# An emission planner with measured durations, a latency per engine, and turns for VectorE and GpSimd

## The chip, the core and the metric

The kernel runs on one core of one Trainium2 chip. The metric is the device time of one execution in microseconds (us), as the median of several runs. Five engines work side by side, each through a queue of its own in the order in which the program was emitted: TensorE (PE in the profile; its weight loads are PEld), VectorE (DVE), ScalarE (ACT), GpSimd (POOL) and SyncE (SP), which here issues the transfers. An instruction waits, by semaphores, for what it reads and for the buffer that it writes, and everything behind it on its queue waits with it.

## The reference

A model of one block of a first kind and two layers of a second kind, on 512 tokens of 1024 columns, all in float32. Cut to what matters here:

```python
def first_block(x, p, ...):
    z = rmsnorm(x, mix_norm) @ w_in                     # 1024 -> 5120
    y_a = pool_mixer(z[..., :1024]) @ w_branch_a        # means over 2, 4, 8, 16 tokens
    y_b = spatial_gating(z[..., 1024:3072]) @ w_branch_b
    x = x + (g_a * y_a + g_b * y_b) @ w_out             # g: sigmoids of the rest of z
    x = x + conv_ffn(rmsnorm(x, ffn_norm), ...)         # 1024 -> 2 x 2816 -> 1024, conv of width 3
    x = x + sigmoid(rmsnorm(x, ple_norm) @ w_ple_gate) * (p @ w_ple)
    return rmsnorm(x, final_norm)

def second_block(x, ...):
    for i in range(2):
        x = x + 0.5 * swiglu(rmsnorm(x, ...), ...)      # 1024 -> 2 x 2816 -> 1024
        h = rmsnorm(x, mix_norm[i])
        x = x + (sliding_window_attention(h, ...) if i == 0 else latent_attention(h, ...))
        x = x + 0.5 * swiglu(rmsnorm(x, ...), ...)
    return x
```

`sliding_window_attention` adds to its scores a bias that depends on the distance of two positions (a table of 32 rows, picked by thresholds). `latent_attention` has 16 heads of 96 columns and a causal mask.

## The kernel before

**Numbers.** Activations lie with columns on partitions and the 512 tokens on the free axis. Each float32 operand is split into two parts that TensorE multiplies exactly (`op`, high and low; `wh` and `wl` for a weight), and a product takes three matmuls for each block of 128 x 128 weights: `wh` with the high part, `wh` with the low part, `wl` with the high part. A projection of 1024 columns to 128 is 8 blocks, 24 matmuls of 512 columns, into one PSUM bank. There are five banks `ps` for these and three banks `pt` for small products.

**Weights** come in chunks of 128 x 1024: a transfer on SP into `wr` (3 buffers), a cast on ScalarE to `wh` and a subtraction on GpSimd to `wl` (4 buffers each, so that three chunks are ahead of the one in use).

**Stages.** `mixer`; `conv_ffn`; `ple`; `final_and_ffn` (the last norm of the first block and a feed-forward); `attn_a` (sliding window); two times `ffn`; `attn_b` (latent); `ffn`. A feed-forward goes through `up_down`: 12 pairs of projections with what stands between them and the operand of the down projection (in `conv_ffn`: a convolution of three tokens for each of the two, a gelu, a product and a split), `down(0)` over the first 11 hidden blocks, 10 pairs, `down(1)` over the other 11. Eleven blocks are 33 matmuls for each of the 8 banks of a down projection.

**A norm** begins with ScalarE's squares of the eight tiles of `x` and VectorE's sum over them (`sumsq`, additions f<-f of two SBUF tiles). TensorE then takes the column sums with `mcol` (four float32 products of one column, `mean_tok`), VectorE makes the reciprocal root from them in twelve small steps and a diagonal matrix, TensorE a product of it with `ones`, and ScalarE copies that (`bcast`). Projections of the stage can start before, since the factor of a token is applied to their result.

**The table of biases** for the sliding window is made during `conv_ffn` in 28 chunks (`plan_bias`, `step`), one with each pair where any are left: two times three instructions on VectorE (`e` from `poshi`, `e` with `poslo`, `g` with `poslo`), 24 small matmuls into a `pt` bank, two additions of the mask `con` on VectorE, and, for each second chunk, stores on SP.

**The order.** The program is traced once with stand-ins; each operation becomes an `Instr` with its dependences and its buffers. `Order.arrange` then plays the program through in time: each engine has a clock, an operation can start when its inputs are done, `LAT` = 150 ns later, and its buffers are free, and of those that can start an engine takes the one that is earliest in the program. `_cost` gives the duration of each. A pool's tag in `SPARE` (`f` 3, `ps` 3, `e` 2) may be taken out of the program's order only while so many buffers more than needed are free; with fewer, it is handed out in the program's order. What comes out is the emission order, and with it each engine's queue. The instruction that the profile names L586 is the one line that emits everything. The costs on which the diff bears are

```python
                return max(n / 2.4 + 0.5, 56.0)
        return (3.4 if o.name == "tensor_copy" else 2.24) * n + 80
```

the first for a matmul of n columns on split operands, the second for GpSimd.

Of the kernel before, what the change touches and what calls it, by code (L numbers as in the profile page):

```python
# [10 lines left out]
F32 = mybir.dt.float32  # L11
# [27 lines left out]
SPARE = {"f": 3, "ps": 3, "e": 2}  # L39


# 1 / (2 pi) in parts of 11 bits
# [7 lines left out]
# ---------------------------------------------------------------- host layout  # L50
# [200 lines left out]
# ------------------------------------------------------------- issue order  # L251
#
# The program is first traced with tiles and views that stand for the real ones,
# then every engine's instructions are put in the order in which a list schedule
# over rough costs would start them, and emitted so.
# [99 lines left out]
class Instr:  # L355
    __slots__ = ("eng", "name", "args", "kw", "deps", "tiles", "cost", "new", "table", "n", "ready", "bytes", "key",
                 "rows")
# [10 lines left out]
class Order:  # L368
    LAT = 150.0
# [13 lines left out]
    def _cost(self, o):  # L383
# [3 lines left out]
        if o.eng == "tensor":  # L387
            if o.name == "transpose":
                return 107.0
            n = math.prod(kw["rhs"].shape[1:])  # L390
            dt = kw["rhs"].dtype
            if dt == F32R:
                return max(n / 2.4 + 0.5, 56.0)
            return 4 * (n / 2.4 + 2.5) if dt == F32 else max(n / 2.4 + 2.5, 27.0)
# [18 lines left out]
        return (3.4 if o.name == "tensor_copy" else 2.24) * n + 80  # L413

    def add(self, eng, name, args, kw):
# [29 lines left out]
        o.cost = self._cost(o)  # L445
        o.rows = kw["rhs"].shape[0] / P if "rhs" in kw else 1.0
# [7 lines left out]
    def arrange(self):  # L454
        import heapq
# [17 lines left out]
        warm, busy, window = False, 0.0, 0.0  # L473
# [8 lines left out]
        def fits(o):  # L482
# [5 lines left out]
            for k, c in need.items():  # L488
                if free[k] < c:
                    return False  # L490
                if free[k] < c + SPARE.get(k[1], 99):
                    f, i = fifo[k], head[k]
                    while c:
                        if id(f[i]) not in placed:
                            if f[i] not in o.new:
                                return False
                            c -= 1
                        i += 1
            return True

        while len(out) < len(self.ops):
# [8 lines left out]
            for e in engines:  # L510
# [44 lines left out]
                clock[e] = now + c  # L555
                end = now + c
# [5 lines left out]
                for x in after[o.n]:  # L562
                    x.ready = max(x.ready, end + (0.0 if x.eng == o.eng == "tensor" else self.LAT))
# [8 lines left out]
            if not nxt:  # L572
                if progress:
                    continue
                stuck = [(e, self.ops[n].name, n, [b.name for b in self.ops[n].new]) for e in engines
                         for _, n in sorted(able[e])[:2]]
                raise RuntimeError(f"no order found: {stuck}")
            now = min(nxt)
        return out
# [10 lines left out]
# ---------------------------------------------------------------- on the chip  # L590
# [37 lines left out]
class Core:  # L628
# [80 lines left out]
    # products of operands in two exact parts  # L709
# [84 lines left out]
    # ------------------------------------------------------------ first block  # L794
# [211 lines left out]
    # ----------------------------------------------------------- second block  # L1006
# [32 lines left out]
    # relative-position bias and mask of the sliding window, one table entry at  # L1039
    # a time by thresholds of the distance  # L1040
# [80 lines left out]
    def attn_a(self):  # L1121
# [13 lines left out]
        # heads of 64 columns brought to length one, in place  # L1135
# [34 lines left out]
        # keys of the two groups side by side, zero where the groups do not meet  # L1170
# [116 lines left out]
    # sine and cosine of position times frequency, by exact reduction in turns  # L1287
# [62 lines left out]
    def attn_b(self):  # L1350
# [7 lines left out]
        # latents and the shared key part, tokens on partitions, two token tiles at a time  # L1358
# [50 lines left out]
        # one over the length of four heads of 96 columns in four token tiles  # L1409
# [79 lines left out]
        # keys of tile st against queries st..3, three banks  # L1489
# [154 lines left out]
```

## Time and profile before

| | |
|---|---|
| median of 3 runs | 2785.83 us (2784.25 to 2788.27) |
| span of the profiled execution | 2782.1 us |
| TensorE busy | 2679.4 us, 96 % of the span |
| VectorE, ScalarE, GpSimd busy | 1376.1, 954.7, 1225.4 us (49, 34, 44 %) |
| read from memory | 242.76 MB, 91 GB/s over the span with what is written |

The profile is of one execution. Its span is the time from the first to the last instruction. Busy time is the time in which an engine works on something; waiting for a semaphore is idle. PEclk is the granted clock of TensorE as a share of its upper level: 1.00 is 2.4 GHz and 0.50 is 1.2 GHz. An arrow in a row is out<-in, by the tiles' names; the shape is partitions x elements.

### The profile page before, as it was taken

Reading aid. Unit: us, or ns where it says so; the run is one execution under the profiler, and the core shown is the slowest. Engines: PE = TensorE matmul, PEld = TensorE weight load, DVE = VectorE, ACT = ScalarE, POOL = GpSimd, SP = SyncE. Lnnn points to the kernel's source line nnn. Section 1 sums busy time; section 2 is a strip of 40 time slices with the busy share of each in tenths; the row PEclk is TensorE's granted clock in tenths of the full one; section 3 lists DMA queues with packets and bytes.
Section 4 is the critical chain, followed back from the end, with each engine's and each line's share of the span. In section 5 each row is a group of like instructions: output and inputs, shape, how many; then the busy total and the mean of one; then the engine's idle time right before and its main releaser. Section 6 shows DMA issues by size and latency. Waiting matters only on the chain. (4 is left out here: it accounts for less than half of the span.)

```text
span 2782.1 us, 32524 instructions
## 1 busy us (share of the span) xinstructions
PE 2679.4 (96%) x12768; PEld 2187.3 (79%) x12768; DVE 1376.1 (49%) x2193; ACT 954.7 (34%) x1486; POOL 1225.4 (44%) x664
## 2 busy tenths in 40 slices
PE   7999998999799899999999999999999899999999
PEld 5788886888677788889778888888888766688887
DVE  5506369949937861335743313343133676533141
ACT  3324333323334222334633223323223475432221
POOL 4543443353334344444534444444444443344443
PEclk9999999999899999999999999999999999999999
DMA  4232223333323333333222233322333201233322
GB/s 148 95 99 89 93 92 102 93 114 106 91 70 97 99 99 98 99 99 105 78 84 93 97 99 99 97 86 97 98 99 96 58 12 31 72 99 99 98 92 83
DMA packets 102617, 254.31 MB, mean 91 GB/s; under 512 B 37360, under 2 KB 39024, under 8 KB 102464
## 3 DMA queue, kind: packets, MB, share of 16 engines
q1 hardware_dynamic: 101840, 250.26, 28.4%
q8 instruction: 101, 1.65, 0.2%
q0 software_dynamic: 624, 1.97, 0.2%
q14 instruction: 52, 0.43, 0.1%
HBM read 242.76 MB, written 9.44 MB: 91 GB/s over the span
## 5 line engine op out<-in xcount | busy, mean ns | idle before, releaser
L586 PE MATMUL ps<-op,wh 128*128 128x512 f32 x6624 | 2069.9, 393 | 35.9 <-ACT op L586 24.4
L586 POOL TENSOR_TENSOR wl<-wr,wh 128x1024 fp32r<-128x1024 f32 (+3 forms) x467 | 1107.6, 2374 | 1393.3 <-ACT wh L586 1380.0
L586 PEld LDWEIGHTS ps<-op,wh 128*128 128x128 f32 x6624 | 1250.5, 189 | 304.7 <-ACT op L586 27.0
L586 PE MATMUL ps<-op,wl 128*128 128x512 f32 x3312 | 1299.7, 392 | 0.0
L586 ACT CAST wh<-wr 128x1024 fp32r<-128x1024 f32 (+3 forms) x471 | 468.1, 994 | 1236.7 <-PE ps L586 760.4
L586 PEld LDWEIGHTS ps<-op,wl 128*128 128x128 f32 x3312 | 627.4, 189 | 132.2 <-issue 1.0
L586 DVE TENSOR_TENSOR f<-ps,f 128x512 f32<-128x512 f32 x260 | 178.8, 688 | 532.9 <-PE ps L586 510.9
L586 DVE TENSOR_TENSOR op<-f,op 128x512 fp32r<-128x512 f32 x136 | 226.2, 1665 | 68.8 <-ACT op L586 68.0
L586 DVE TENSOR_TENSOR f<-f 128x512 f32<-128x512 f32 x213 | 203.1, 954 | 46.0 <-POOL f L586 19.8
L586 DVE SCALAR_TENSOR_TENSOR x<-ps,x 128x512 f32<-128x512 f32 x64 | 44.2, 691 | 339.0 <-PE ps L586 339.0
L586 ACT CAST op<-f 128x512 fp32r<-128x512 f32 x136 | 84.2, 621 | 211.1 <-DVE f L586 211.1
L586 PE MATMUL ps<-wh,op 128*128 128x256 f32 (+3 forms) x608 | 149.9, 333 | 4.8 <-ACT f L586 2.5
L586 PEld LDWEIGHTS ps<-wh,op 128*128 128x128 f32 x608 | 106.0, 194 | 15.6 <-ACT f L586 3.1
L586 ACT ACTIVATE f<-f 128x512 f32<-128x512 f32 x142 | 89.0, 627 | 77.8 <-DVE f L586 77.1
L586 DVE SCALAR_TENSOR_TENSOR f<-f,vec 128x512 f32<-128x512 f32 x88 | 104.5, 1188 | 8.9 <-ACT f L586 8.6
L586 DVE SCALAR_TENSOR_TENSOR op<-x,vec,op 128x512 fp32r<-128x512 f32 x64 | 84.4, 1324 | 48.1 <-ACT op L586 48.1
L586 PE MATMUL ps<-wl,op 128*128 128x256 f32 (+3 forms) x304 | 100.4, 330 | 0.0
L586 DVE TENSOR_TENSOR x<-ps,x 128x512 f32<-128x512 f32 x56 | 38.4, 688 | 98.6 <-PE ps L586 98.6
L586 ACT ACTIVATE op<-x,vec 128x512 fp32r<-128x512 f32 x64 | 45.8, 721 | 73.1 <-DVE x L586 72.8
L586 PE MATMUL pt<-con,opf 128*128 128x128 f32 (+1 forms) x348 | 54.5, 280 | 8.2 <-DVE opf L586 3.5
L586 PEld LDWEIGHTS ps<-wl,op 128*128 128x128 f32 x304 | 59.0, 194 | 3.5 <-issue 0.3
L586 DVE TENSOR_TENSOR g<-e,poslo 128x512 bf16<-128x512 f32 x56 | 61.4, 1098 | 0.1
(181 smaller groups left out, 1366.1 us busy)
## 6 DMA issues: line engine op xcount, KB each, us to landing
wr<-in_w SPq DMA_DIRECT2D x411, 512.0 KB, 3.3
wr<-in_w SPq DMA_DIRECT2D x40, 256.0 KB, 2.7
bias<-e SPq DMA_DIRECT2D x28, 256.0 KB, 2.7
opf<-bias SPq DMA_DIRECT2D x16, 448.0 KB, 6.0
x<-in_xT SPq DMA_DIRECT2D x8, 256.0 KB, 6.7
out_y<-x SPq DMA_DIRECT2D x8, 256.0 KB, 2.0
wr<-in_w SPq DMA_DIRECT2D x4, 416.0 KB, 3.1
wr<-in_w SPq DMA_DIRECT2D x12, 128.0 KB, 2.1
```

What stands on the lines that cost most here:

```text
L586: getattr(getattr(self.nc, o.eng), o.name)(*[real(a) for a in o.args], **{k: real(v) for k, v in o.kw.items()})
```

## The change

No operation of the program is added, removed or altered. What changes is the model by which `arrange` plays it through, and so the order of each queue.

- `LAT` becomes a number for each engine on which the operation ran that is waited for: 203 ns for TensorE, 111 VectorE, 128 ScalarE, 90 GpSimd, 34 SP.
- Costs: a split matmul of 512 columns goes from 213.8 to 227.0 ns, one float32 product and one bf16 product change by a few ns, a GpSimd operation from 2.24 to 2.35 ns an element (a copy from 3.4 to 2.0), with 60 for 80 ns around it.
- `_port` marks all of GpSimd's operations and those VectorE operations that read two SBUF sources, or copy or scale from SBUF to SBUF. Marked operations share one more clock: none starts in the plan before the last marked one has ended.
- `arrange` tries several times: where the play-through comes to a point at which nothing can start, the tags that hold it up get one more spare in `SPARE`, and it starts anew. With these costs it ends at `f` 7, `ps` 7, `e` 2. Five `ps` banks and 7 spares mean that `ps` banks are handed out in the program's order throughout.

Some comments go as well, so that the emitting line is L617.

```diff
-    LAT = 150.0
+    LAT = {"tensor": 203.0, "vector": 111.0, "scalar": 128.0, "gpsimd": 90.0, "sync": 34.0}
...
-                return max(n / 2.4 + 0.5, 56.0)
-            return 4 * (n / 2.4 + 2.5) if dt == F32 else max(n / 2.4 + 2.5, 27.0)
+                return max(n / 2.4 + 13.7, 56.0)
+            return 4 * (n / 2.4 + 1.0) if dt == F32 else max(n / 2.4 + 2.0, 28.0)
...
-        return (3.4 if o.name == "tensor_copy" else 2.24) * n + 80
+        return (2.0 if o.name == "tensor_copy" else 2.35) * n + 60
+
+
+    def _port(self, o):
+        if o.eng == "gpsimd":
+            return o.name != "dma_start"
+        if o.eng != "vector" or o.name == "memset":
+            return False
+        vs = [v for v in list(o.kw.values()) + list(o.args) if isinstance(v, View) and self._size(v) > 1]
+        near = [v for v in vs if not v.base.pool.pool_psum]
+        if o.name in ("tensor_copy", "tensor_scalar"):
+            return len(near) == len(vs)
+        return o.name in ("tensor_tensor", "scalar_tensor_tensor", "tensor_tensor_reduce") and len(near) > 2
...
     def arrange(self):
+        spare = dict(SPARE)
+        for _ in range(40):
+            left = {id(b): b.left for o in self.ops for b in o.tiles}
+            out, stuck = self._arrange(spare)
+            if not stuck:
+                return out
+            for o in self.ops:
+                for b in o.tiles:
+                    b.left = left[id(b)]
+            for tag in stuck:
+                if tag in spare:
+                    spare[tag] += 1
+        raise RuntimeError(f"no order found: {stuck}")
+
+    def _arrange(self, spare):
...
-                if free[k] < c + SPARE.get(k[1], 99):
+                if free[k] < c + spare.get(k[1], 99):
...
-                clock[e] = now + c
-                end = now + c
+                begin = now
+                if o.port:
+                    begin = max(now, port)
+                    port = begin + c
+                clock[e] = begin + c
+                end = begin + c
...
-                    x.ready = max(x.ready, end + (0.0 if x.eng == o.eng == "tensor" else self.LAT))
+                    x.ready = max(x.ready, end + (0.0 if x.eng == o.eng == "tensor" else self.LAT[o.eng]))
```

TensorE, at the norm ahead of the last feed-forward: its column sums stand in the row with `mcol`; `ps_18374` before and `ps_18367` after are the first projection of the stage, `ps_18401` the second. Before:

```order
L586 MATMUL ps_18374<-op_18308,wh_18295 128x512 x2
L586 MATMUL ps_18374<-op_18308,wl_18305 128x512
L586 MATMUL ps_18374<-op_18335,wh_18295 128x512 x2
L586 MATMUL pt_18405<-mcol_86,f_18212 128x1 x4
L586 MATMUL ps_18374<-op_18335,wl_18305 128x512
L586 MATMUL ps_18374<-op_18357,wh_18295 128x512 x2
```

After:

```order
L617 MATMUL ps_18367<-op_18364,wh_18296 128x512
L617 MATMUL ps_18401<-op_18204,wh_18319 128x512 x2
L617 MATMUL ps_18401<-op_18204,wl_18328 128x512
...
L617 MATMUL ps_18401<-op_18281,wh_18319 128x512 x2
L617 MATMUL pt_18428<-mcol_86,f_18208 128x1 x4
L617 MATMUL ps_18401<-op_18281,wl_18328 128x512
```

The sum stood behind 17 matmuls of the stage and now stands behind 35, the first projection and half of the second.

VectorE, at the last pair of the convolution: `op_5814` before and `op_5818` after is the low part of the pair's operand, for which the down projection waits; rows with `poshi`, `poslo` or `con` belong to chunks of the table of biases. Before:

```order
L586 TENSOR_TENSOR e_5771<-pt_5740,con_133 128x8x32
L586 TENSOR_TENSOR e_5777<-pt_5740,con_133 128x8x32
L586 TENSOR_TENSOR g_5781<-e_5712,poslo_2999 128x512
L586 SCALAR_TENSOR_TENSOR f_5774<-f_5499,vec_84,f_5774 128x512
L586 TENSOR_TENSOR e_5736<-e_5736,poslo_2999 128x512
L586 SCALAR_TENSOR_TENSOR f_5774<-f_5499,vec_84,f_5774 128x512
L586 TENSOR_TENSOR g_5781<-e_5736,poslo_2999 128x512
L586 TENSOR_TENSOR f_5708<-f_5708,f_5774 128x512
L586 TENSOR_TENSOR op_5814<-f_5708,op_5814 128x512
```

After:

```order
L617 SCALAR_TENSOR_TENSOR f_5782<-f_5775,vec_84,f_5782 128x512
L617 TENSOR_TENSOR e_5800<-poshi_3005 128x512
L617 SCALAR_TENSOR_TENSOR f_5782<-f_5775,vec_84,f_5782 128x512
L617 TENSOR_TENSOR e_5800<-e_5800,poslo_3023 128x512
L617 TENSOR_TENSOR f_5753<-f_5753,f_5782 128x512
L617 TENSOR_TENSOR g_5815<-e_5800,poslo_3023 128x512
L617 TENSOR_TENSOR e_5822<-poshi_3005 128x512
L617 TENSOR_TENSOR op_5818<-f_5753,op_5818 128x512
L617 TENSOR_TENSOR e_5822<-e_5822,poslo_3023 128x512
```

The last chunk's second half and its two additions of `con` stood ahead of the last operand and now stand behind it.

TensorE, at the start of the second down projection, which needs that operand: `ps_5766` before and `ps_5661` after is its first bank; `ps_5822` before and `ps_5706`, `ps_5791` after are later ones. Before:

```order
L586 MATMUL ps_5766<-op_5685,wh_5618 128x512 x2
L586 MATMUL ps_5766<-op_5685,wl_5650 128x512
L586 MATMUL ps_5822<-op_4288,wh_5618 128x512
L586 MATMUL ps_5766<-op_5814,wh_5618 128x512
L586 MATMUL ps_5822<-op_4288,wh_5618 128x512
```

After:

```order
L617 MATMUL ps_5706<-op_5741,wl_5616 128x512
L617 MATMUL ps_5791<-op_4341,wh_5607 128x512 x2
...
L617 MATMUL ps_5791<-op_5324,wh_5656 128x512 x2
...
L617 MATMUL ps_5661<-op_5818,wh_5547 128x512
L617 MATMUL ps_5706<-op_5818,wh_5607 128x512
L617 MATMUL ps_5791<-op_5324,wl_5670 128x512
```

Ahead of the first matmul on the last operand stood 31 matmuls of the down projection, and now stand 80, over three banks.

## Rows read from the trace of the kernel before

**Rows 1.** The page's head and its part 1: busy time, share, instructions

```profile
span 2782.1 us, 32524 instructions
...
PE 2679.4 (96%) x12768; PEld 2187.3 (79%) x12768; DVE 1376.1 (49%) x2193; ACT 954.7 (34%) x1486; POOL 1225.4 (44%) x664
```

**Rows 2.** The chain in order of time: start, length, engine, tile, instructions

```profile
1825.74 351.37 PE ps L586 x1550
```

**Rows 3.** The table of TensorE's waits: us in total, times, longest

```profile
PE ps L586 <- ACT op L586: 24.8, 6, 14.6
PE pt L586 <- DVE g L586: 11.8, 6, 4.5
PE ps L586 <- ACT wh L586: 10.3, 2, 8.5
```

**Rows 4.** TensorE's groups by form: count, busy, mean ns, idle before and releaser

```profile
L586 PE MATMUL pt<-mcol,f 128*128 128x1 f32 x80 | 14.4, 301 | 28.6 <-DVE f L586 28.6
```

**Rows 5.** Stretches: length, busy PE PEld DVE ACT POOL, PEclk, DMA share, GB/s

```profile
0.00:45.00 45.00, 26.13 (x83) 19.22 (x84) 25.86 (x48) 18.16 (x28) 20.85 (x16) 0.89 0.53 181
430.00:480.00 50.00, 38.99 (x235) 30.80 (x236) 48.33 (x65) 13.70 (x18) 18.88 (x7) 0.93 0.34 99
741.00:766.00 25.00, 8.21 (x23) 5.53 (x22) 21.52 (x27) 8.59 (x12) 7.48 (x3) 0.59 0.26 83
878.00:925.00 47.00, 38.52 (x177) 30.20 (x176) 30.63 (x59) 13.09 (x19) 12.34 (x6) 0.78 0.20 62
1447.00:1462.00 15.00, 9.70 (x36) 7.57 (x35) 8.56 (x21) 4.61 (x7) 6.41 (x3) 0.77 0.22 70
2200.00:2240.00 40.00, 29.36 (x135) 22.71 (x133) 34.18 (x111) 25.46 (x61) 18.83 (x39) 0.87 0.11 32
2240.00:2400.00 160.00, 157.61 (x772) 103.57 (x773) 104.74 (x246) 91.78 (x237) 66.43 (x111) 1.00 0.11 31
2411.00:2425.00 14.00, 7.55 (x26) 6.06 (x25) 9.15 (x21) 2.72 (x4) 4.82 (x3) 0.63 0.26 77
```

**Rows 6.** Timeline of the first norm: start, length, instruction, [idle before <-releaser]

```profile
12.55 0.68 DVE L586 TENSOR_TENSOR f<-f 128x512 f32<-128x512 f32 x1
...
18.77 12.84 DVE L586 TENSOR_TENSOR f<-f 128x512 f32<-128x512 f32 x5
...
19.96 11.11 POOL L586 TENSOR_TENSOR wl<-wr,wh 128x1024 fp32r<-128x1024 f32 x4
...
31.67 1.87 PE L586 MATMUL pt<-mcol,f 128*128 128x1 f32 x8 [6.75 <-DVE f L586]
```

**Rows 7.** One stretch behind that wait, columns as in rows 5

```profile
31.67:38.20 6.53, 6.53 (x19) 5.51 (x20) 2.84 (x16) 0.00 (x0) 0.00 (x0) 0.50 0.27 80
```

**Rows 8.** Timeline between the two norms at 878 to 925

```profile
901.65 9.41 DVE L586 TENSOR_TENSOR f<-f 128x512 f32<-128x512 f32 x7
...
911.12 1.87 PE L586 MATMUL pt<-mcol,f 128*128 128x1 f32 x8 [5.30 <-DVE f L586]
...
915.40 0.88 DVE L586 TENSOR_SCALAR f<-con,rtok 128x128 f32<-128x128 f32 x4
```

**Rows 9.** VectorE's groups by form in 430 to 750, columns as in rows 4

```profile
L586 DVE SCALAR_TENSOR_TENSOR f<-f,vec 128x512 f32<-128x512 f32 x79 | 95.7, 1212 | 5.3 <-ACT f L586 5.0
L586 DVE TENSOR_TENSOR g<-e,poslo 128x512 bf16<-128x512 f32 x44 | 44.4, 1009 | 0.0
L586 DVE TENSOR_TENSOR e<-e,poslo 128x512 f32<-128x512 f32 x45 | 43.4, 965 | 0.0
L586 DVE TENSOR_TENSOR e<-poshi 128x512 f32<-128x512 f32 x45 | 37.0, 826 | 0.0
...
L586 DVE TENSOR_TENSOR e<-pt,con 128x256 f32<-128x256 f32 x40 | 14.9, 411 | 1.5 <-PE pt L586 1.5
```

**Rows 10.** The chain in order of time, second attention: one head's maximum and exponentials

```profile
2250.18 1.06 DVE bmx L586 x2
...
2253.77 1.65 ACT opf L586 x6
```

More of the change, by code (lines that the diff above doesn't have):

```diff
@@ L356 @@
     __slots__ = ("eng", "name", "args", "kw", "deps", "tiles", "cost", "new", "table", "n", "ready", "bytes", "key",
-                 "rows")
+                 "rows", "port")
 class Engine:
@@ L445, in add @@
         o.cost = self._cost(o)
+        o.port = self._port(o)
         o.rows = kw["rhs"].shape[0] / P if "rhs" in kw else 1.0
@@ L472, in arrange @@
         table, dma = None, 0.0
-        warm, busy, window = False, 0.0, 0.0
+        warm, busy, window, port = False, 0.0, 0.0, 0.0
         done = []
@@ L574, in arrange @@
                     continue
-                stuck = [(e, self.ops[n].name, n, [b.name for b in self.ops[n].new]) for e in engines
-                         for _, n in sorted(able[e])[:2]]
-                raise RuntimeError(f"no order found: {stuck}")
+                return out, sorted({b.slot[1] for e in engines for _, n in sorted(able[e])[:2] for b in self.ops[n].new})
             now = min(nxt)
-        return out
+        self.end, self.spare = now, spare
+        return out, []
     def emit(self):
```

## The prediction

> **What bounds the kernel now.** I read the busy shares first: the span is 2782.1 us and TensorE is busy in 2679.4 of it [rows 1]. So the question is the 102.7 us in which TensorE does nothing, and the time in which it runs slowly. How fast it can go shows in the chain: one piece of 1550 matmuls in a row takes 351.37 us, 226.7 ns each [rows 2]. The table of waits then says whom TensorE waits for: 24.8 us for ScalarE's `op`, 14.6 of them at once, 11.8 us for VectorE's `g`, 10.3 us for the weight `wh` (two waits at the start of the kernel) [rows 3]. The costliest wait is for VectorE's tile `f` at one kind of instruction, the column sums with `mcol` that begin a norm: 28.6 us of idle time stand ahead of them [rows 4]. The table by stretches gives the places [rows 5]: TensorE is idle 18.9 us of the first 45, 11.0 of 430:480 (the convolution's first pairs, which share VectorE with the table of biases), 16.8 of 741:766 (their end), 8.5 of 878:925 (two norms behind each other), 5.3 of 1447:1462, 10.6 of 2200:2240 (start of the second attention) and 6.5 of 2411:2425. That is 77.6 of the 102.7 us.
>
> Why these waits are there, the first one shows [rows 6]. VectorE adds two SBUF tiles in 0.68 us at 12.55 us. From 18.77 us five such additions take 12.84 us, 2.57 each, while GpSimd makes four weight remainders in 11.11 us. Each addition waits for about one GpSimd instruction. TensorE has taken up the sum in its queue and stands for 6.75 us although it has other matmuls. The planner of before does not know of this and puts the sum too early. Behind that wait TensorE is busy throughout 31.67:38.20, at a granted clock of 0.50, 1.2 GHz [rows 7]; half of these 6.5 us is lost, 3.3. The mean clock of 0.63 in 2411:2425 [rows 5] tells of the same behind a wait of 6.45 us there, and I take 3.0.
>
> **The change, part by part.** No instruction is added or removed; only the order on each queue moves. Terms are us of TensorE's time, from one execution with a span of 2782.1; the median of the runs is 2785.83, so I take 3.7 us around the span as given and subtract from the median.
>
> *Norms.* The sum moves back on TensorE behind matmuls that are ready. At the start by 41 matmuls: the wait of 6.75 us and the 3.3 us of slow clock go. Against it, a cast of a weight is put behind one more square (0.6), and a sum that comes later makes all five `ps` banks full before the norm's factor arrives, which I put at 0.4. Term 9.0. Ahead of the last feed-forward by 18, 18 x 226.7 ns = 4.1 of 6.45 us [rows 5]; there and at 1453 VectorE's last `x` is now updated ahead of the queued additions. With two thirds of the 3.0 us of slow clock: 6.0. At 1453 by 20 matmuls, 4.5 of 5.3 us, and I add 1.5 of slow clock: 6.0. The other sums share 28.6 - 6.75 - 5.30 - 5.30 - 6.45 = 4.8 us [rows 4] in four places and move by 4 to 9 matmuls (0.9 to 2.0 us): 4.8, and 1.7 for a slow stretch behind one of them, as long as that of a short wait can be, an estimate from rows 7. Together 27.5.
>
> *The two norms at 878:925* are different, since there TensorE runs out of banks. Between them lie eight products on `x` and seven additions on VectorE, the additions alone 9.41 us [rows 8], which the change leaves in their order. TensorE has five banks of 24 matmuls, 27.2 us, and the planner now uses them up, so that the second sum and the product with `ones` stand next to each other and TensorE waits between them. What is gained is that this product no longer stands behind 18 matmuls at half clock, 18 x 2 x 0.2267 = 8.2 us, but is reached when VectorE is ready: its factor is on the diagonal at 916.28, 3.3 us after the sum ended at 912.99 [rows 8]. That is 4.9, and I take 4.5, bounds 0 and 8.5, all idle time there.
>
> *First pairs of the convolution.* Per pair VectorE needs four products of 1.21 us [rows 9] and four lighter instructions, which I put at the 0.68 us of an undisturbed addition [rows 6]: 7.6. A chunk of the bias table is twice 0.97 + 0.83 + 1.01 + 0.41 us [rows 9]: 6.4. TensorE needs 48 x 0.2267 = 10.9 us per pair and about 0.9 for a chunk. A pair with a chunk is 14.0 against 11.8: VectorE can't follow, and TensorE stands at `g`. The change puts a chunk's products two to three projections later and moves two whole chunks (12.8 us of VectorE) from the pairs into the down projection behind them. That covers the 11.0 us idle, but TensorE's and VectorE's loads up to there come out nearly equal, so I leave a third: 7.5, with 2.5 of the 3.5 us that a granted clock of 0.93 over 50 us takes [rows 5]. Term 10, bounds 0 and 14.5.
>
> *End of the pairs.* TensorE stands 14.6 us for the last pair's `op` [rows 3], 16.8 us with the waits just before [rows 5]. Ahead of it the plan of before has 31 matmuls of the down projection, that of after 80, over three banks. The 49 more are 11.1 us. On VectorE four chunk instructions go behind the last `op`, 0.97 + 1.01 + two of 0.41 = 2.8 us [rows 9]. 13.9 of 16.8; with 0.6 of slow clock 14.5, bounds 0 and 19.
>
> *Attention.* The planner gives up at its first spares and ends with 7 for `f` and for `ps`. There are five `ps` banks, so they are handed out strictly in the program's order, where before a later product could take a bank early. At 2200:2240 projections of the next group (eight of 512 columns and three of 384, some 2.4 us) now come behind the first head's scores. I charge 3, bounds -3 (a gain, since waits of 10.6 us are there) and 10.
>
> *Stores on SP.* SP waits for VectorE's `e` with each chunk of the table, and weight loads stand behind. TensorE waits for `wh` only twice [rows 3], both at the start, so the three chunks loaded ahead (3 x 24 x 0.2267 = 16 us) hide it. The stores move behind two to six more loads: nothing, as long as no such wait passes 16 us.
>
> Sum: 27.5 + 4.5 + 10 + 14.5 - 3 = 53.5. 2785.8 - 53.5 = 2732.3.
>
> The Trainium skill, TensorE: Matmul & The Clock Gate (Part 1: The HAM clock gate), has 215.7 ns from start to start for a warm matmul of 512 columns. The planner of before holds 213.8 and that of after 227. The rows have 226.7. By the page the 128 moved matmuls would cover 1.4 us less, and the sum would be 52.
>
> **The rivals.** *The port stays the bound* in the convolution. GpSimd's instructions still come when a weight is cast, whatever the plan says; VectorE still waits, its work per pair and chunk is still 14.0 us against 11.8, and TensorE's waits at 430:480 and 741:766 come back behind other instructions. For it: VectorE is busy 48.3 of 50 us there [rows 5]. Against it: it has room in the down projection between, which the new order fills. The terms 10 and 14.5 fall away: 2732.3 + 24.5 = 2756.8. The Trainium skill, SBUF — State Buffer (Who interferes with whom), says that issue order decides who blocks and that the other waits a whole instruction; by that rule a turn can be moved but not removed, which is this rival. Rows 6 agree with whole instructions.
>
> *Strict banks cost more than all the rest gains.* At 2240:2400 TensorE is busy 157.6 of 160 us [rows 5], since other products run while a head's maximum (1.06 us for two on VectorE) and exponentials (1.65 on ScalarE) are made [rows 10]. If heads can no longer overlap because a bank may not be taken early, each of 16 shows these 2.7 us and the semaphores between, perhaps 3.6: 58 us. It decides from 53.5 / 16 = 3.3 us a head. Against it: in the new order two heads still stand interleaved with projections. 2732 + 58 = 2790.
>
> *The plan is moved but not the waits:* VectorE's additions also come later (they stand behind more `op`), so that TensorE stands at the same instructions as before. Then all terms fall away and 2783 to 2788 remain. Against it: the stretches have ready matmuls that were behind the waits.
>
> *All of it:* the conv waits go whole and the attention gains its 3: 4.5 + 4.5 + 6 + 3 more, 2714; with a further 6 of the second attention's 10.6 us, 2708.
>
> **How the numbers follow.** Forecast 0.62, port 0.20, all of it 0.09, moved but not the waits 0.05, strict banks 0.04. The range 2708 to 2762 holds the first three but for their edges; the upper end is the port rival with another 5 us for attention. What this kernel's measurement can tell is about 0.2%, 5.6 us: faster by more 0.91, within 0.05, slower 0.04.
>
> **What would show it.** In the profile after: idle time ahead of the `mcol` products under 15 instead of 28.6 us (it stays where the two norms are), no wait of TensorE above 5 us in 741:766's place, waits for `g` under 4 us, granted clock 0.98 or more at the start of the last feed-forward; TensorE's busy time about 2665, less by the slow stretches. Waits for `op` above 15 us would speak for the port; 20 us more idle time in the second attention for strict banks. Wrong would be the whole if VectorE's additions come later by as much as the sums do.

## The result, and the profile after

The changed kernel takes 2721.84 us (median of 4 runs, 2720.72 to 2722.23), the kernel before in the same rounds 2787.05 us. The ratio is 0.9767, 95 % interval 0.9753 to 0.9781: 65.2 us or 2.3 % faster. 2732 was forecast, 53.5 us faster.

The head and part 1 of the page after, beside [rows 1]:

```profile
span 2719.0 us, 32505 instructions
...
PE 2659.2 (98%) x12768; PEld 2167.5 (80%) x12768; DVE 1399.1 (51%) x2193; ACT 954.9 (35%) x1486; POOL 1238.4 (46%) x664
```

TensorE is idle for 59.8 instead of 102.7 us, and its same 12768 matmuls take 20.2 us less, since fewer of them run at the lower clock (the mean granted clock of the execution is 0.983 before and 0.994 after). That is the whole of the 63.1 us between the two spans. VectorE, though, is busy 23 us longer than before.

TensorE's waits after (us in total, times, longest), the first six, beside [rows 3]:

```profile
PE pt L617 <- DVE f L617: 10.2, 3, 6.3
PE ps L617 <- ACT wh L617: 9.3, 4, 8.0
PE pt L617 <- POOL opf L617: 6.7, 6, 2.2
PE ps L617 <- ACT op L617: 6.3, 3, 3.3
PE ps L617 <- DVE amx L617: 3.7, 2, 3.3
PE pt L617 <- DVE g L617: 3.5, 3, 2.0
```

The 14.6 us for the last pair's `op` are gone, `g` went from 11.8 to 3.5 us. Of the norms' sums one still waits, the second of the two that follow each other (group of TensorE by form, beside [rows 4]):

```profile
L617 PE MATMUL pt<-mcol,f 128*128 128x1 f32 x80 | 10.8, 256 | 6.3 <-DVE f L617 6.3
```

The same places as in [rows 5], shifted by what was gained ahead of them (length, busy PE, PEld, DVE, ACT, POOL, granted clock, DMA share, GB/s):

```profile
0.00:45.00 45.00, 34.08 (x132) 25.45 (x133) 27.40 (x45) 20.28 (x30) 25.66 (x18) 1.00 0.60 205
420.00:480.00 60.00, 60.00 (x346) 48.79 (x346) 49.74 (x71) 20.50 (x25) 29.75 (x12) 1.00 0.32 102
480.00:560.00 80.00, 72.90 (x426) 57.46 (x425) 75.02 (x111) 28.70 (x36) 34.71 (x12) 0.96 0.32 94
705.00:750.00 45.00, 45.00 (x260) 36.54 (x260) 39.84 (x55) 18.96 (x25) 20.17 (x8) 1.00 0.33 102
838.00:893.00 55.00, 45.21 (x229) 36.56 (x228) 44.59 (x74) 19.91 (x28) 16.60 (x7) 0.88 0.24 75
1395.00:1410.00 15.00, 15.00 (x72) 12.52 (x71) 13.04 (x19) 6.74 (x9) 8.97 (x4) 1.00 0.46 144
2140.00:2185.00 45.00, 34.22 (x160) 23.94 (x158) 36.03 (x120) 29.99 (x72) 23.89 (x48) 0.92 0.16 46
2185.00:2345.00 160.00, 154.56 (x753) 100.18 (x754) 103.84 (x245) 88.24 (x225) 63.72 (x103) 1.00 0.09 28
2352.00:2366.00 14.00, 14.00 (x67) 11.73 (x66) 11.97 (x21) 5.53 (x9) 7.62 (x4) 1.00 0.44 131
```

At the end of the pairs (705:750) and at the norms ahead of two feed-forwards (1395:1410, 2352:2366) TensorE no longer stops, and its clock stays at 2.4 GHz. The first pairs of the convolution are covered up to 480, but 7.1 us of idle time came back between 480 and 560. The two norms (838:893) and the start of the second attention (2140:2185) wait as before; among the attention's heads behind it (2185:2345) TensorE is idle 5.4 us, where the kernel before has 2.4 (2240:2400).

What the start shows is the core of the case (timeline, beside [rows 6]):

```profile
11.89 0.68 DVE L617 TENSOR_TENSOR f<-f 128x512 f32<-128x512 f32 x1
...
18.12 13.00 DVE L617 TENSOR_TENSOR f<-f 128x512 f32<-128x512 f32 x5
...
19.30 16.52 POOL L617 TENSOR_TENSOR wl<-wr,wh 128x1024 fp32r<-128x1024 f32 x6
...
33.44 0.95 PE L617 MATMUL pt<-mcol,f 128*128 128x1 f32 x8
```

VectorE's five additions take 13.00 us where they took 12.84: GpSimd blocks them as before. But TensorE takes up the sum at 33.44 us without a wait, because other matmuls stand ahead of it.

A table by stage follows from VectorE's updates of `x` (the time from the last update of one stage to that of the next; the second half of an attention's output stands with the feed-forward behind it, since the wait for the norm lies across that border). The second half of each of the four swiglu feed-forwards takes 168.6 us in both kernels.

| stage | before | after | difference | forecast |
|---|---|---|---|---|
| mixer | 399.3 | 390.0 | -9.3 | -9.0 |
| convolution, first pairs and `down(0)` | 219.6 | 213.4 | -6.1 | -10 |
| convolution, other pairs and `down(1)` | 197.4 | 177.5 | -19.9 | -14.5 |
| `ple`, first and third feed-forward | 64.7 + 213.1 + 195.3 | 61.3 + 208.8 + 192.4 | -10.6 | -4.5 - 6.5 |
| first attention, first half | 161.1 | 157.7 | -3.4 | 0 |
| its second half, second feed-forward | 221.7 | 214.0 | -7.7 | -6.0 |
| second attention, first half | 194.7 | 198.6 | +3.9 | +3 |
| its second half, last feed-forward | 237.5 | 227.4 | -10.1 | -6.0 |

### The profile page after: what moved, and what is told of

It reads as the page before. It is cut to its first block, busy times and chain, and to the rows that moved or that the text cites. A ratio compares the mean times of both kernels' runs of the same rounds, so it can differ in the third digit from the quotient of the medians.

```text
span 2719.0 us, 32505 instructions
## 1 busy us (share of the span) xinstructions
PE 2659.2 (98%) x12768; PEld 2167.5 (80%) x12768; DVE 1399.1 (51%) x2193; ACT 954.9 (35%) x1486; POOL 1238.4 (46%) x664
## 4 chain that ended last, share of the span: by engine, by line
PE 49%; DVE 1%; ACT 1%; issue 0%; POOL 0%; ACTq 0%; DVEq 0%
PE ps L617 48%; PE pt L617 2%; ACT opf L617 1%; ACT e L617 0%; DVE bmx L617 0%; ACT f L617 0%; DVE rst L617 0%; DVE e L617 0%; DVE bssq L617 0%; POOL opf L617 0%; DVE op L617 0%; DVE opf L617 0%; DVE f L617 0%; DVE bssk L617 0%; ACT wh L617 0%
## 5 line engine op out<-in xcount | busy, mean ns | idle before, releaser
L617 PE MATMUL ps<-op,wh 128*128 128x512 f32 x6624 | 2057.5, 391 | 17.8 <-ACT wh L617 9.3
L617 POOL TENSOR_TENSOR wl<-wr,wh 128x1024 fp32r<-128x1024 f32 (+3 forms) x467 | 1119.0, 2397 | 1315.0 <-ACT wh L617 1307.7
L617 PEld LDWEIGHTS ps<-op,wh 128*128 128x128 f32 x6624 | 1242.5, 188 | 281.5 <-ACT wh L617 10.6
L617 PE MATMUL ps<-op,wl 128*128 128x512 f32 x3312 | 1293.5, 391 | 0.1
L617 ACT CAST wh<-wr 128x1024 fp32r<-128x1024 f32 (+3 forms) x471 | 469.2, 996 | 1352.7 <-PE ps L617 810.3
L617 PEld LDWEIGHTS ps<-op,wl 128*128 128x128 f32 x3312 | 623.5, 188 | 131.4 <-issue 2.2
L617 DVE TENSOR_TENSOR f<-ps,f 128x512 f32<-128x512 f32 x260 | 178.1, 689 | 498.8 <-PE ps L617 476.9
L617 DVE TENSOR_TENSOR op<-f,op 128x512 fp32r<-128x512 f32 x136 | 241.9, 1779 | 73.4 <-ACT op L617 72.8
L617 DVE TENSOR_TENSOR f<-f 128x512 f32<-128x512 f32 x213 | 204.4, 962 | 30.7 <-POOL f L617 11.1
L617 DVE SCALAR_TENSOR_TENSOR x<-ps,x 128x512 f32<-128x512 f32 x64 | 44.3, 692 | 335.4 <-PE ps L617 335.4
L617 PE MATMUL ps<-wh,op 128*128 128x256 f32 (+3 forms) x608 | 148.3, 329 | 4.2 <-ACT f L617 1.9
L617 ACT CAST op<-f 128x512 fp32r<-128x512 f32 x136 | 84.2, 621 | 113.9 <-DVE f L617 113.7
L617 DVE SCALAR_TENSOR_TENSOR op<-x,vec,op 128x512 fp32r<-128x512 f32 x64 | 94.9, 1493 | 43.6 <-ACT op L617 43.6
L617 PEld LDWEIGHTS ps<-wh,op 128*128 128x128 f32 x608 | 103.8, 190 | 16.6 <-issue 4.6
L617 PE MATMUL ps<-wl,op 128*128 128x256 f32 (+3 forms) x304 | 98.8, 325 | 0.0
L617 DVE SCALAR_TENSOR_TENSOR f<-f,vec 128x512 f32<-128x512 f32 x88 | 91.4, 1050 | 13.2 <-ACT f L617 13.1
L617 ACT ACTIVATE f<-f 128x512 f32<-128x512 f32 x142 | 88.7, 626 | 26.9 <-DVE f L617 26.6
L617 PE MATMUL pt<-con,opf 128*128 128x128 f32 (+1 forms) x348 | 56.4, 284 | 13.2 <-POOL opf L617 6.7
L617 DVE TENSOR_TENSOR x<-ps,x 128x512 f32<-128x512 f32 x56 | 38.3, 686 | 51.9 <-PE ps L617 51.9
L617 ACT ACTIVATE op<-x,vec 128x512 fp32r<-128x512 f32 x64 | 45.6, 720 | 53.4 <-DVE x L617 53.1
L617 POOL TENSOR_TENSOR opf<-opf,bden 128x384 f32<-128x384 f32 (+2 forms) x48 | 31.0, 672 | 68.7 <-DVE bden L617 68.7
L617 PEld LDWEIGHTS pt<-con,opf 128*128 128x128 f32 (+1 forms) x348 | 39.5, 138 | 27.2 <-POOL opf L617 8.3
```

The costliest lines, as they stand in the source:

```text
L617: getattr(getattr(self.nc, o.eng), o.name)(*[real(a) for a in o.args], **{k: real(v) for k, v in o.kw.items()})
```

## The experiments

The theory at the outset: on the chip the two engines block each other after the change as before; the gain is that the plan knows it and puts TensorE's waiting instructions behind matmuls that are ready. Its rivals: the measured durations and latencies make the gain; handing out the banks in the program's order makes it; the turns make the blocking itself less; the port bounds the kernel whatever the order.

### Turns alone

```diff
-    LAT = {"tensor": 203.0, "vector": 111.0, "scalar": 128.0, "gpsimd": 90.0, "sync": 34.0}
+    LAT = {"tensor": 150.0, "vector": 150.0, "scalar": 150.0, "gpsimd": 150.0, "sync": 150.0}
...
-                return max(n / 2.4 + 13.7, 56.0)
+                return max(n / 2.4 + 0.5, 56.0)
...
-        return (2.0 if o.name == "tensor_copy" else 2.35) * n + 60
+        return (3.4 if o.name == "tensor_copy" else 2.24) * n + 80
```

(against the kernel after; the float32 and bf16 products get their old costs too)

> The changed planner with the old costs and one latency of 150 ns, so that of the change only the turns of VectorE and GpSimd (and the retry that they need; it ends at spares of 7 for f and ps) are left. If the turns bring the gain, at least three quarters of the 65 us stay: 2720 to 2738. If the measured durations and latencies bring it, 2775 to 2790.

Measured: 2748.1 us, ratio 0.9863 (0.9848 to 0.9877). That is 38 of the 65 us, between the two expectations. The turns are needed, but the rest of the numbers matter with them. What is late now is the second of the two norms (timeline of TensorE):

```profile
887.92 1.87 PE L617 MATMUL pt<-mcol,f 128*128 128x1 f32 x8 [12.17 <-DVE f L617]
...
893.22 2.04 PE L617 MATMUL pt<-f,ones 128*128 128x512 f32 x2 [3.43 <-DVE f L617]
```

It waits 12.17 us, in the kernel after 6.31.

### All but the turns

```diff
     def _port(self, o):
-        if o.eng == "gpsimd":
-            return o.name != "dma_start"
+        return False
```

> The changed planner with the measured durations and the latency per engine, but with no operation marked for turns; the spares then stay at 3, 3, 2. If the turns bring the gain: 2775 to 2790, with the sums of the norms still waited for, 25 us or more ahead of the mcol products. If the durations and latencies bring it: 2720 to 2740.

Measured: 2791.25 us, ratio 1.0020 (1.0011 to 1.0030). Better durations and latencies alone are worth nothing, or a little less. By stages the first halves of the two attentions are longer than before, 167.6 instead of 161.1 and 197.6 instead of 194.7 us, although the spares are the old ones. The sums wait as they did in [rows 4]:

```profile
L616 PE MATMUL pt<-mcol,f 128*128 128x1 f32 x80 | 14.6, 304 | 30.6 <-DVE f L616 30.5
```

### The spares alone

```diff
-SPARE = {"f": 3, "ps": 3, "e": 2}
+SPARE = {"f": 7, "ps": 7, "e": 2}
```

(against the kernel before)

> The kernel before with spares of 7 for f and ps, which the changed planner ends with; nothing else. It tells what handing out the banks in the program's order does by itself. My prediction charged 3 us for it in the second attention: 2786 to 2793 by that. The measured kernel was 9 us faster over both attentions; if strict banks are the cause of this, 2774 to 2780. If neither, within 3 us of 2786.

Measured: 2788.75 us, ratio 1.0014 (1.0004 to 1.0023). The larger spares, of `f` as of the banks, cost 3 us in the kernel as a whole. By stages the first half of the second attention is 5.2 us longer, where the change costs 3.9, and the mixer and the convolution's first part 2.7 and 2.9; the first attention gains nothing by it (+1.3 us). The stages come from one execution each, and the spans of these two lie 7.7 us apart where the medians lie 2.8 apart, so that differences of this size are not certain. Strict banks are no cause of the gain.

### The sums later, without turns

```diff
+                    late = 3500.0 if getattr(x.kw.get("rhs"), "base", None) is self.mcol else 0.0
-                    x.ready = max(x.ready, end + (0.0 if x.eng == o.eng == "tensor" else self.LAT[o.eng]))
+                    x.ready = max(x.ready, end + late + (0.0 if x.eng == o.eng == "tensor" else self.LAT[o.eng]))
```

(against a planner with the old costs and latency and no turns)

> The planner of before in costs, latency and without turns, but each norm's column sums are planned 3.5 us later than their input is ready (the retry ends at spares of 7). It tells whether it is enough that TensorE takes up the sums later. If the gain at the norms is that TensorE has matmuls ahead of the sum, the norms ahead of the feed-forwards gain as in the changed kernel (3 to 5 us each in four stages, 12 to 20 in all) and the convolution keeps its waits: 2762 to 2775. If it is VectorE's order that counts, 2783 or more.

Measured: 2812.53 us, ratio 1.0092 (1.0077 to 1.0107), slower than either expectation. Half of the theory holds: the second, third and last feed-forward, with the attention's second half ahead of it where there is one, gain 2.7, 2.9 and 5.0 us against before, and the idle time at the sums falls to 15.3 us. But the convolution's first part is 10.5 us slower, the first feed-forward 9.2 and the second attention's first half 15.2. The spares are those of the run before; they account for 2.9 of the 10.5 and 5.2 of the 15.2 us, if its stages are taken as they stand, and the rest is the delay's doing. TensorE's group of the sums, and two rows of its table of waits:

```profile
L617 PE MATMUL pt<-mcol,f 128*128 128x1 f32 x80 | 12.3, 228 | 15.3 <-DVE f L617 15.3
```

```profile
PE pt L617 <- DVE f L617: 29.0, 10, 11.3
PE pt L617 <- DVE g L617: 19.9, 12, 6.1
```

11.3 us at one sum, the second of the two norms in a row, and 19.9 instead of 11.8 us for `g`: one added number for all norms repairs some waits and makes others. Why the delay of a sum lengthens the waits for `g` was not settled.

### Which of the numbers

Turns and TensorE's measured durations only:

```diff
-    LAT = {"tensor": 203.0, "vector": 111.0, "scalar": 128.0, "gpsimd": 90.0, "sync": 34.0}
+    LAT = {"tensor": 150.0, "vector": 150.0, "scalar": 150.0, "gpsimd": 150.0, "sync": 150.0}
...
-        return (2.0 if o.name == "tensor_copy" else 2.35) * n + 60
+        return (3.4 if o.name == "tensor_copy" else 2.24) * n + 80
```

> Turns, and of the measured durations those of TensorE alone (227 instead of 213.8 ns for a matmul); GpSimd's old costs and 150 ns for all latencies. Turns alone gave 2748, all of it 2722, so 26 us hang on numbers that without turns gave nothing (2791). If it is that a plan whose TensorE is 6 per cent too fast puts the sums behind too many matmuls (the second of the two norms then waits 12 instead of 6 us), most of it is here: 2722 to 2732. If it is the latencies or GpSimd's costs, 2742 to 2750.

Turns and all measured durations, with one latency:

```diff
-    LAT = {"tensor": 203.0, "vector": 111.0, "scalar": 128.0, "gpsimd": 90.0, "sync": 34.0}
+    LAT = {"tensor": 150.0, "vector": 150.0, "scalar": 150.0, "gpsimd": 150.0, "sync": 150.0}
```

> Turns and all measured durations, with 150 ns for all latencies: all of the change but its latency per engine. If TensorE's duration is what counts, this lies within 5 us of the run with turns and TensorE's durations, and within 5 of the whole change: 2719 to 2730. If the latencies make the attention's 9 us, 2730 to 2740.

Measured: 2726.23 us (ratio 0.9783, 0.9768 to 0.9798) and 2734.8 us (0.9813, 0.9799 to 0.9828). So the ladder is, each step with turns: 2748 with the old numbers, 2726 with TensorE's durations, 2735 with GpSimd's as well, 2722 with the latencies. In the plan of the first run TensorE is 6 % too fast. That costs 22 us in all, and a part of it shows in the wait at the second norm, 12.17 us there and 6.3 with the measured duration:

```profile
L617 PE MATMUL pt<-mcol,f 128*128 128x1 f32 x80 | 10.8, 256 | 6.3 <-DVE f L617 6.3
```

It is the same row as in the kernel after. GpSimd's costs then make it 9 us worse, and the latencies bring 13, of which 9.0 lie in the attentions: 5.6 in the first half of the first (163.3 to 157.7 us) and 3.4 in the second. In the first the granted clock rises (a stretch over that attention, of the run with one latency and then of the kernel after):

```profile
1230.00:1412.00 182.00, 169.74 (x1118) 146.84 (x1118) 108.40 (x328) 93.75 (x247) 82.47 (x68) 0.97 0.26 90
```

```profile
1225.00:1400.00 175.00, 166.47 (x1108) 143.98 (x1108) 106.29 (x327) 93.57 (x247) 80.61 (x67) 0.99 0.28 91
```

### Is the blocking still there, and what does it cost?

```diff
-            (nc.vector if first else nc.gpsimd).tensor_tensor(out=lo[:, c], in0=raw[:, c], in1=h[:, c].bitcast(F32),
-                                                              op=ALU.subtract)
+            if first:
+                nc.vector.tensor_tensor(out=lo[:, c], in0=raw[:, c], in1=h[:, c].bitcast(F32), op=ALU.subtract)
+            else:
+                nc.gpsimd.memset(lo[:, c].bitcast(F32), 0.0, _a=raw[:, c], _b=h[:, c])
```

(the two last arguments are for the planner alone, which gets the old cost and the old dependences)

> The changed kernel in exactly its order, but GpSimd fills each weight remainder wl with zeros instead of subtracting two SBUF tiles; the remainder's share of the products is left out of the result by that, and GpSimd reads nothing there. VectorE's additions of two SBUF tiles should fall from a mean of 962 ns to about 690 and its busy time from 1399 to under 1250 us, which shows that the longer time is waiting for GpSimd. If the new order covers nearly all that is left of the blocking, the time falls by 5 to 15 us (the waits for f and g, 14 us with what slow clock they bring): 2707 to 2717. If the port still bounds the convolution, as one of the rivals had it, by 25 or more: under 2697.

Measured: 2697.92 us, ratio 0.9682 (0.9668 to 0.9697), 24 us less than the kernel after in the same order. The page's part 1, and two groups of VectorE by form:

```profile
PE 2651.4 (98%) x12768; PEld 2164.0 (80%) x12768; DVE 1025.9 (38%) x2193; ACT 951.5 (35%) x1486; POOL 541.3 (20%) x664
```

```profile
L619 DVE TENSOR_TENSOR f<-f 128x512 f32<-128x512 f32 x213 | 147.8, 695 | 32.0 <-ACT f L619 15.4 <-POOL f L619 6.7
L619 DVE TENSOR_TENSOR op<-f,op 128x512 fp32r<-128x512 f32 x136 | 94.5, 695 | 91.8 <-ACT op L619 91.2
```

The kernel after has for the same two, and then the kernel before:

```profile
L617 DVE TENSOR_TENSOR op<-f,op 128x512 fp32r<-128x512 f32 x136 | 241.9, 1779 | 73.4 <-ACT op L617 72.8
L617 DVE TENSOR_TENSOR f<-f 128x512 f32<-128x512 f32 x213 | 204.4, 962 | 30.7 <-POOL f L617 11.1 <-ACT f L617 9.5
```

```profile
L586 DVE TENSOR_TENSOR op<-f,op 128x512 fp32r<-128x512 f32 x136 | 226.2, 1665 | 68.8 <-ACT op L586 68.0
L586 DVE TENSOR_TENSOR f<-f 128x512 f32<-128x512 f32 x213 | 203.1, 954 | 46.0 <-POOL f L586 19.8 <-ACT f L586 16.1
```

An addition needs 695 ns; it takes 954 before, 962 after. The turns in the plan do not make the blocking less: VectorE spends 373 us (1399.1 - 1025.9) on it, more than before (350 by the same subtraction, 1376.1 - 1025.9). What they do is to hide it: of 373 us, 24 are left in the end. By stages most of it lies in the convolution's first part (8.5 us), the two norms with their feed-forward (5.3), the mixer (5.0) and the second attention's first half (4.4). The time lies between the two expectations and all but at that of the port as a bound (under 2697): the new order covers much less of the rest than I expected. That GpSimd doesn't hinder VectorE where it only writes agrees with the Trainium skill, SBUF — State Buffer (Who interferes with whom).

### The two norms

```diff
-        r1 = self.bcast(self.rstd_tok())
+        y1 = self.rstd_tok()
...
+            nc.scalar.activation(out=q, in_=self.x[j], func=AF.Square, scale=self.v("fin", j))
...
+        self.mul(v2, ps[:, 0:4], y1)
+        self.mul(v2, v2, y1)
...
+        rB = self.bcast(y2)
+        r1 = self.bcast(y1)
...
-        rB = self.bcast(self.rstd_tok())
-        self.mul(rB, rB, r1)
```

> The changed kernel, with the second of the two norms that follow each other taken from the old x: the squares are of x times the gain of the first norm, so that both sums are made side by side, and the mean is multiplied by the square of the first factor before the root. As many squares and additions, and the update of x no longer lies between the norms. The changed kernel waits 6.3 and 3.4 us there and then runs 13.7 us at the lower clock, of which a part is those waits. If that is all: 12 to 15 us less, 2707 to 2711. If the banks run out all the same before the second factor is there: 2715 to 2722.

Measured: 2708.53 us, ratio 0.9722 (0.9706 to 0.9739), 13.3 us less than the kernel after; the first feed-forward alone is 13.6 us shorter. The stretch that had 45.21 us of matmuls in 55 at a clock of 0.88 is now full:

```profile
838.00:893.00 55.00, 55.00 (x310) 44.91 (x309) 51.19 (x86) 22.78 (x32) 24.02 (x10) 1.00 0.31 98
```

So what was waited for there is the chain from the first sum to the second factor, which is longer than five banks of matmuls; the orders tried here didn't hide it, a shorter chain did.

### Taking the blocking away

All weight remainders are subtracted on VectorE, by the same edit in four kernels: the one with one sum for both norms, the kernel before, the kernel after, and the kernel before with one sum for both norms.

```diff
-            (nc.vector if first else nc.gpsimd).tensor_tensor(out=lo[:, c], in0=raw[:, c], in1=h[:, c].bitcast(F32),
+            nc.vector.tensor_tensor(out=lo[:, c], in0=raw[:, c], in1=h[:, c].bitcast(F32),
```

> The kernel with one sum for both norms (2708.5), with all weight remainders subtracted on VectorE, so that GpSimd no longer blocks it there. The blocking was 373 us of VectorE's busy time in the run without GpSimd's reads and cost 24 us in the end. A remainder of 1024 columns should take VectorE some 1.3 us, twice an addition of 695 ns, 550 us in all. If blocking is worse than the work itself: 2690 to 2705. If VectorE then bounds the convolution, where a pair with a chunk and its two remainders comes to more than TensorE's 11.8 us: 2715 to 2750.

> The kernel before, with its old planner, and one edit: all weight remainders are subtracted on VectorE, so that GpSimd reads little there. If the gain of the change is that its plan knows of the blocking, the old plan is good enough once there is no blocking: at most 10 us above the run with the new planner and the same edit. If the measured durations and latencies or VectorE's order are worth something by themselves, 20 us or more above it.

> The changed kernel, and the same edit (both norms summed one after the other, as there). With one sum for both norms it was 2694.4; with the wait between the norms back, of 10 to 13 us by the run that took it out: 2700 to 2708.

> The old planner with the weight remainders on VectorE (2691.1), and one sum for both norms. What is left of the wait between the norms there is 3.5 us and 3.4 us at the lower clock: 2685 to 2689. If the old planner, which knows nothing of latencies measured, loses as much elsewhere: within 2 us of 2691.

| planner | norms | remainders on | us | ratio (interval) |
|---|---|---|---|---|
| new | one sum | VectorE | 2694.42 | 0.9671 (0.9655 to 0.9687) |
| old | as before | VectorE | 2691.07 | 0.9661 (0.9646 to 0.9675) |
| new | as before | VectorE | 2698.77 | 0.9688 (0.9671 to 0.9704) |
| old | one sum | VectorE | 2686.40 | 0.9643 (0.9627 to 0.9659) |

The old planner with one line changed beats the new one with the same line by 7.7 us (their intervals overlap slightly, but in the same rounds the runs lie at 2690.80 to 2691.30 and at 2697.86 to 2699.71), and the kernel after by 31. The new planner with the norms as before was expected at 2700 to 2708: it lies only 4.4 us above its run with one sum, since the sums wait no more there either (0.5 us in all). Part 1 of the page of that kernel, and its remainders and sums (groups by form, of VectorE and of TensorE):

```profile
PE 2651.9 (99%) x12768; PEld 2167.5 (81%) x12768; DVE 1532.8 (57%) x2660; ACT 954.3 (35%) x1486; POOL 123.4 (5%) x197
```

```profile
L586 DVE TENSOR_TENSOR wl<-wr,wh 128x1024 fp32r<-128x1024 f32 x411 | 505.4, 1230 | 266.5 <-ACT wh L586 265.4
```

```profile
L586 PE MATMUL pt<-mcol,f 128*128 128x1 f32 x80 | 9.5, 240 | 0.0
```

The same remainders on GpSimd, in the kernel before:

```profile
L586 POOL TENSOR_TENSOR wl<-wr,wh 128x1024 fp32r<-128x1024 f32 x411 | 1032.5, 2514 | 1279.6 <-ACT wh L586 1266.2 <-PE ps L586 13.2
```

A remainder takes VectorE 1230 ns and GpSimd 2514, 2.04 times as long; the Trainium skill, GPSIMD Engine Reference (4.1 Engine selection), puts elementwise work on two inputs at about twice. 505 us of new work on VectorE take the place of its waiting, and no sum is waited for, with a plan that knows nothing of turns. In the convolution's stretches VectorE is busy 130.5 of 140 us and TensorE doesn't stop:

```profile
420.00:480.00 60.00, 60.00 (x365) 48.62 (x365) 55.75 (x91) 24.01 (x31) 0.00 (x0) 1.00 0.32 97
480.00:560.00 80.00, 80.00 (x464) 64.94 (x464) 74.79 (x129) 27.50 (x34) 0.00 (x0) 1.00 0.41 126
```

The test of the theory is the pair of rows in the middle of the table, from the same rounds: without the blocking, what the new planner knows is worth nothing. It even loses, nearly all in the second attention's first half (197.8 against 191.0 us), where its spares end at 5 and the banks are handed out in order again; whether that is the cause is not shown, since the new numbers lengthen this stage with the old spares too (197.6 us in the run without turns). The old planner with both edits is at 2686.40 us the fastest of all, 99 us under the kernel before; that it is better than the one without the second edit is not secured, since the two intervals overlap.

## Why the prediction came out as it did

**Direction and reason** were right: the idle time lay in TensorE's waits, the sums and the last operand were moved behind ready matmuls, and the signs that were named all showed: 6.3 us ahead of the sums, at the two norms only; no wait over 5 us at the end of the pairs; 3.5 us for `g`; clock 1.00 at the last feed-forward; TensorE busy 2659 where about 2665 was put. The gain was 65.2 us and 53.5 was forecast. Three terms were too small, the end of the pairs by 5.4 us, the norms behind the attentions by 5.8 and the first attention by 3.4; the first pairs were put 3.9 too high, and the others came within 1 us.

**Start**: 9.0 forecast, 9.3 measured. The wait of 6.75 us and the slow stretch behind it are gone, as the prediction said (the orders move the sum by 43 matmuls, from 36 to 79, and not by 41, which changes nothing here). That the sum came so near is in part luck. Over the stage TensorE's idle time fell by 7.9 us (22.2 to 14.3), since the waits for `wh` got shorter too (10.3 to 9.3), where 0.6 had been charged for a later cast, and its busy time by only 1.3 (377.1 to 375.8) and not by 3.3: a later wait of 3.33 us, which both kernels have, now has a slow stretch behind it. The stretches from the end of that wait, before and after:

```profile
128.57:135.00 6.43, 6.43 (x28) 5.33 (x29) 3.45 (x5) 3.79 (x6) 2.21 (x1) 1.00 0.21 76
```

```profile
117.46:124.00 6.54, 6.54 (x21) 4.95 (x22) 3.54 (x5) 3.92 (x6) 2.40 (x1) 0.74 0.20 72
```

**Norms behind the attentions**: 6.0 each forecast, 7.7 and 10.1 measured. The term was mis-sized in one step. I let only as much of the wait go as the sum had moved (18 matmuls, 4.1 of 6.45 us), and two thirds of the slow clock. But VectorE's last update of `x` also came sooner, which I had seen in the order and not priced. In the kernel before, that update stood behind an addition that took 2.82 us; now the updates stand ahead of the additions. Before and after, at the last feed-forward:

```profile
2412.54 2.82 DVE L586 TENSOR_TENSOR f<-f 128x512 f32<-128x512 f32 x1
2415.29 0.68 DVE L586 TENSOR_TENSOR x<-ps,x 128x512 f32<-128x512 f32 x1
```

```profile
2355.51 0.68 DVE L617 TENSOR_TENSOR x<-ps,x 128x512 f32<-128x512 f32 x1
2356.11 3.19 DVE L617 SCALAR_TENSOR_TENSOR op<-x,vec,op 128x512 fp32r<-128x512 f32 x2
2359.22 2.20 DVE L617 TENSOR_TENSOR f<-f 128x512 f32<-128x512 f32 x3
```

```profile
2361.95 0.95 PE L617 MATMUL pt<-mcol,f 128*128 128x1 f32 x8
```

The additions end at 2361.42 and TensorE takes up the sum at 2361.95: the whole wait and the whole slow stretch are gone. With 226.7 ns for each of the 17 and 35 matmuls of the stage that stand ahead of the sum, I estimate that its input was ready 10.2 us after the attention's last matmul before and 7.4 after. These 2.8 us are the step that was not priced; with the 4.1 they cover the wait of 6.45.

**Other norms and the two in a row**: 11.0 together, 10.6 measured. (1.8 of the waits counted here stand at the norms of the convolution and of the second attention, in other rows of the table.) The two norms still wait, as forecast, and the run with one sum shows why.

**Convolution**: 24.5 forecast, 26.0 measured, but as the sum of two errors. The end of the pairs gave 19.9 instead of 14.5: nothing was left of the 16.8 us of idle time, of which I had let 13.9 go, and the slow clock behind the wait gave 3.1 and not 0.6 (busy 180.6 to 177.5). The first pairs gave 6.1 instead of 10: 7.1 us of idle time came back after 480, so that 6.0 and not 7.5 us went, and of the 2.5 us for the clock nothing came (busy 206.4 and 206.3), since the slow stretch moved with the wait (0.96 over 480:560). The run without GpSimd's reads takes 8.5 us off just this part.

**Attention**: +3 was charged for strict banks and the second attention's first half took 3.9 us more, but that strict banks are the reason is not shown. The spares alone lengthen it by 5.2 us and the new numbers with the old spares by 2.9, so that either would do; and the added idle time lies among the heads, while the idle time at 2140:2185, where I had placed it, stayed. What the sum left out is the first attention, -3.4 us, for which I had no term. Beside the turns the latencies per engine are worth 5.6 us there, and I had never costed them by themselves; without turns the same numbers made this stage 6.5 us longer. Why they gain only together stays open.

**The rivals**: strict banks fell (3 us by themselves); the waits that only move fell too, except in the second part of the first pairs. That of the port had its premise right and its outcome wrong: the blocking goes on in full, but the convolution, where the rival had no gain at all, gained 26.0 us. Of what the blocking still costs in the end, 24 us, only 8.5 lie in the convolution; that 24 is near the rival's 24.5 is chance, since that was the gain it denied.

## What to carry over

When two engines block each other, first ask whether the slower one needs the work at all: one line that moved it to an engine with room for it (VectorE is busy 57 % of the time with it) was worth more here than a planner that knows of the blocking, and it worked with the old plan. A plan that puts an in-order engine's waiting instruction behind ready work hides the wait without shortening it; look at the blocked engine's mean durations to tell the two apart. And constants of a planner don't add up: durations and latencies that gave nothing alone gave 26 us beside the turns, though one part of them, GpSimd's costs, lost 9.

## What the runs showed of the hardware

An instruction of four columns waits as long as a large one. In the kernel after (timeline of one norm's chain on VectorE and of GpSimd):

```profile
846.14 2.39 POOL L617 TENSOR_TENSOR wl<-wr,wh 128x1024 fp32r<-128x1024 f32 x1 [6.20 <-ACT wh L617]
...
846.18 2.37 DVE L617 TENSOR_SCALAR rsi<-msv 128x4 int32<-128x4 int32 x1
...
848.59 0.17 DVE L617 TENSOR_SCALAR rtok<-rsi 128x4 int32<-128x4 int32 x1
```

The next of the same form takes 0.17 us. The first reads one tile from SBUF, not two, and began 0.04 us after GpSimd's instruction. So a norm's chain of small steps loses 2.2 us for each one that starts just behind a weight remainder.
